# The attention output product as seven block products for eight, with its sums prepared in DRAM

## The chip, the cores and the metric

The kernel runs on one core of one Trainium2 chip. The metric is the device time of one execution in microseconds (us); lower is better. Before the change three runs gave 892.99, 893.65 and 893.84 us. A core has the engines TensorE (PE, with its weight loads shown as PEld), VectorE (DVE), ScalarE (ACT), GpSimd (POOL) and SyncE (SP). SP issues most transfers (DMAs); GpSimd issues those that add onto their destination.

## The reference, cut to what matters

One encoder layer on 512 tokens of width 1024, in float32: two mixers (a state-space scan and a gated spatial mixer), then cross-attention to 256 memory tokens, then a SwiGLU feed-forward layer of width 2816, each added onto the residual stream `h`, and a last norm.

```python
def memory_cross_attention(hn, memn, w_q, w_k, w_v, w_o):
    q = (hn @ w_q).reshape(bsz, seq, XATTN_HEADS, XATTN_HEAD_DIM)   # 4 heads of 256
    k = (memn @ w_k).reshape(bsz, MEM_LEN, XATTN_HEADS, XATTN_HEAD_DIM)
    v = (memn @ w_v).reshape(bsz, MEM_LEN, XATTN_HEADS, XATTN_HEAD_DIM)
    p = jax.nn.softmax(einsum('blhd,bmhd->bhlm', q, k) * XATTN_HEAD_DIM ** -0.5, axis=-1)
    o = jnp.einsum('bhlm,bmhd->blhd', p, v).reshape(bsz, seq, D_MODEL)
    return o @ w_o                                                  # w_xo, 1024 x 1024
...
h = h + memory_cross_attention(rms_norm(h, xattn_norm_g), memn, w_q, w_k, w_v, w_xo)
h = h + swiglu(rms_norm(h, ffn_norm_g), w_gate, w_up, w_down)
```

The change concerns `o @ w_o`, its addition onto `h`, and transfers for `w_q` and `w_down`.

## The kernel before, in words

**Three passes.** Each float32 operand is split into a high part (`split`, L85: a ScalarE cast to a shorter format) and a low part (L86: VectorE subtracts the high part). A product is three matmuls, high x high, high x low, low x high (`mm3`, L358). So each weight block costs TensorE matmuls, ScalarE one cast and VectorE one subtraction, and each product operand made on the chip the same pair.

**The plan of weights.** `plan` lists all weight blocks in the order of use. `next_w` hands out the next block, starts the loads of the blocks ahead of it (`LOADS` = 3 blocks; some 4 to 7) and splits up to `SPLITS` = 2 blocks ahead. A block of 128 x 1024 elements (512 KB) is loaded by SP into one of three `wraw` buffers and split into one of three `whi` and `wlo` pairs; some blocks have tiles of their own (`sums_place`). A `wraw` buffer is free when its split is done, a `whi`/`wlo` pair when its matmuls are done.

**Block products.** Several products (w_proj_b, w_q, gate and up, w_down) already use a scheme of the Strassen kind: the matrix is cut into 2 x 2 blocks, and seven products of sums of blocks take the place of eight. Sums of weight blocks that several steps need are made in DRAM by `plan_sums`: at plan entry j SP copies one block to DRAM scratch (L274, held in program order), and at entry j + step GpSimd's queue adds the other block by an accumulating transfer (L275). The list of pairs (j, step) fixes the entries.

**Order.** The program is written as one stream per stage; a scheduler orders each engine's queue at build time, from dependences and its own estimate of durations. Where the program says so (`in_order`), the written order is kept. On the chip each queue issues in its built order and an instruction waits for its operands.

**The stage around the change.** After the w_q product, `scores`, `turn` and `values` make each head's softmax, its transposes and its output; `values` splits the PSUM result into `ot_hi` and `ot_lo`. The w_xo product runs token by token, in two halves of 512 output columns: for the first half `tokm` holds four PSUM banks, for the four tiles of 128 tokens, while heads 1 to 3 are still made between its blocks (hooks `second` and `last_two`); the second half is a loop over token pairs. `add_evac` adds each finished bank onto `h` (L1294) and sums squares on ScalarE (L486). When a token tile has both halves, `feat_norm` norms it: GpSimd takes a root (`r`, L497), VectorE scales (`xs`, L512), TensorE transposes (`ptr`, L520), and ScalarE and VectorE split into `fn`, the operand of the feed-forward layer; `full` keeps the float32 value. The feed-forward stage begins with a remainder of 256 gate columns (`pf<-fn,s`) and the first unit (`px<-fn,whi`).

**Plan entries.** w_xo is plan entries 94 to 101; the feed-forward layer begins at 102.

## Time and profile before

| | |
|---|---|
| median of 3 runs | 893.65 us (892.99 to 893.84) |
| profiled execution | 893.12 us, span 891.3 us, granted TensorE clock 0.997 |
| instructions | 14796 |
| HBM read, written | 157.61 MB, 46.63 MB |

How to read the rows. A row of instructions gives start, duration, engine, line of the kernel, operation, result<-operands by the program's names, shapes, and xN when N follow one another; in brackets stands how long the engine had been idle before and what ended that. Durations of neighbours overlap a little, as instructions are pipelined. A row of waits gives the total in us, how often, and the longest. A row by stretch gives its bounds and length, then each engine's busy time with its number of instructions, the clock granted to TensorE, the mean busy share of the 16 DMA engines and GB/s. A row of transfers ends in the median us from issue to landing.

### The profile page before, as it was taken

What the parts mean: (1) busy time and instruction counts of PE and PEld (TensorE: products, weight loads), DVE (VectorE), ACT (ScalarE), POOL (GpSimd) and SP (SyncE); (2) the same over time, 40 slices, a digit from 0 to 9 for tenths busy, and PEclk for the clock granted to TensorE, in tenths of its full rate; (3) what the DMA queues carried; (4) which work ended last, traced back from release to release, by engine and by line L of the source; (5) the groups of instructions that cost most, each with busy time, mean ns of one, the idle gap of its engine ahead of it and who ended that gap; (6) DMA issues with size and microseconds to landing.
All of it is one profiled execution on the core that took longest, in us unless ns stands there. A gap on an engine that the chain in (4) does not pass through costs nothing.

```text
span 891.3 us, 14796 instructions
## 1 busy us (share of the span) xinstructions
PE 881.1 (99%) x5744; PEld 788.0 (88%) x5744; DVE 642.5 (72%) x1048; ACT 487.4 (55%) x714; POOL 106.9 (12%) x165
## 2 busy tenths in 40 slices
PE   9999999999999999999999999999999999999996
PEld 6788888888889998889899978999999999988875
DVE  5697653889847368658856836676878777899875
ACT  5743994244396254347656534645555455655664
POOL 1005301111032111001001001101121111000010
PEclk9999999999999999999999999999999999999998
DMA  8667456978533789834579747627899999356672
GB/s 255 196 189 182 114 155 177 189 191 190 159 87 84 212 285 268 288 117 140 168 221 256 194 103 197 166 81 181 213 237 233 216 225 249 95 167 207 204 230 102
DMA packets 118408, 165.36 MB, mean 186 GB/s; under 512 B 11825, under 2 KB 84161, under 8 KB 118210
## 3 DMA queue, kind: packets, MB, share of 16 engines
q1 hardware_dynamic: 97474, 135.74, 47.9%
q0 software_dynamic: 20576, 28.15, 19.9%
q8 instruction: 45, 0.74, 0.3%
q10 hardware_dynamic: 288, 0.52, 0.2%
q14 instruction: 25, 0.20, 0.1%
HBM read 157.61 MB, written 46.63 MB: 229 GB/s over the span
## 4 chain that ended last, share of the span: by engine, by line
PE 97%; DMA 1%; SPq 1%; ACT 0%; DVE 0%; issue 0%; POOLq 0%; ACTq 0%
PE pf L358 26%; PE pt L358 17%; PE px L1110 12%; PE dx L358 6%; PE pq L1110 6%; PE dq L358 3%; PE pv L1110 3%; PE bx L1110 3%; PE qx L1110 2%; PE dv L358 2%; PE pz L871 2%; PE pk L814 2%; PE bq L1110 1%; PE qv L1110 1%; PE psc L358 1%; PE qq L1110 1%
## 5 line engine op out<-in xcount | busy, mean ns | idle before, releaser
L86 DVE TENSOR_TENSOR wlo<-wraw,whi 128x1024 fp32r<-128x1024 f32 (+1 forms) x145 | 172.2, 1189 | 101.2 <-ACT whi L85 101.0
L85 ACT CAST whi<-wraw 128x1024 fp32r<-128x1024 f32 (+1 forms) x145 | 148.6, 1026 | 152.2 <-PE pf L358 44.0
L358 PE MATMUL pf<-xn,whi 128*128 128x512 f32 x448 | 139.6, 391 | 0.0
L358 PEld LDWEIGHTS pf<-xn,whi 128*128 128x128 f32 x448 | 83.7, 188 | 17.0
L358 PE MATMUL pf<-xn,wlo 128*128 128x512 f32 x224 | 87.3, 390 | 0.0
L1110 PE MATMUL px<-fn,whi 128*128 128x256 f32 x480 | 83.4, 277 | 0.0
L1110 PEld LDWEIGHTS px<-fn,whi 128*128 128x128 f32 x480 | 72.7, 188 | 0.2
L85 ACT CAST whi<-b 128x1024 fp32r<-128x1024 f32 x40 | 42.2, 1055 | 50.4 <-PE px L1110 27.4
L86 DVE TENSOR_TENSOR wlo<-b,whi 128x1024 fp32r<-128x1024 f32 x40 | 48.9, 1223 | 27.0 <-ACT whi L85 27.0
L1110 PE MATMUL px<-fn,wlo 128*128 128x256 f32 x240 | 66.4, 277 | 0.0
L1110 PE MATMUL pq<-s,whi 128*128 128x256 f32 x320 | 55.0, 276 | 0.0
L358 PE MATMUL dx<-whi,s 128*128 128x512 f32 x170 | 53.4, 390 | 0.4 <-DVE h L1734 0.4
L85 ACT CAST whi<-t 128x1024 fp32r<-128x1024 f32 x30 | 31.6, 1054 | 35.6 <-PE pv L1110 12.4
L86 DVE TENSOR_TENSOR wlo<-t,whi 128x1024 fp32r<-128x1024 f32 x30 | 36.7, 1225 | 19.7 <-ACT whi L85 19.7
L358 PEld LDWEIGHTS pf<-xn,wlo 128*128 128x128 f32 x224 | 42.1, 188 | 8.7
L1110 PEld LDWEIGHTS pq<-s,whi 128*128 128x128 f32 x320 | 48.3, 188 | 0.0
L1110 PEld LDWEIGHTS px<-fn,wlo 128*128 128x128 f32 x240 | 45.1, 188 | 0.0
L358 PE MATMUL pt<-whi,xn 128*128 128x512 f32 x128 | 43.7, 412 | 0.7 <-ACT xn L85 0.7
L1110 PE MATMUL pq<-s,wlo 128*128 128x256 f32 x160 | 44.2, 276 | 0.0
L358 PEld LDWEIGHTS dx<-whi,s 128*128 128x128 f32 x170 | 31.8, 188 | 7.5 <-issue 0.8
L358 PE MATMUL dx<-wlo,s 128*128 128x512 f32 x85 | 33.0, 390 | 0.0
L275 POOL DMA_DIRECT2D dsum<-in_w_down_dram x12 | 13.3, 1105 | 162.4 <-DMA dsum<-in_w_down_dram 162.4
(453 smaller groups left out, 2296.8 us busy)
## 6 DMA issues: line engine op xcount, KB each, us to landing
wraw<-in_w_in_dram SPq DMA_DIRECT2D x36, 512.0 KB, 4.7
dsum<-in_w_down_dram SPq DMA_DIRECT2D x20, 512.0 KB, 5.4
wraw<-dsum SPq DMA_DIRECT2D x20, 512.0 KB, 4.1
b<-in_w_gate_dram SPq DMA_DIRECT2D x15, 512.0 KB, 5.4
b<-in_w_up_dram SPq DMA_DIRECT2D x15, 512.0 KB, 5.3
wraw<-in_w_down_dram SPq DMA_DIRECT2D x15, 512.0 KB, 4.4
dsum<-in_w_down_dram POOLq DMA_DIRECT2D x10, 512.0 KB, 8.1
dsum<-dsum POOLq DMA_DIRECT2D x10, 512.0 KB, 8.5
```

Of the source, the lines that this page charges most:

```text
L85: hi = nc.scalar.copy(dst_hi, src)
L86: lo = nc.vector.tensor_tensor(dst_lo, src, dst_hi.bitcast(F32), ALU.subtract)
L275: plan[j + step][1].append((0, lambda d=dst, x=more: nc.gpsimd.dma_start(d, x, accum_op=ALU.add)))
L358: m = nc.tensor.matmul(ps, a[x], b[y], start=start and i == 0, stop=stop and i == 2, skip_group_check=free)
L814: nc.tensor.matmul(ps[32 * j:32 * j + 32, q, :], bd[i][:, g].rearrange("p d c -> p (d c)"), lc(es[i], g), start=(i == 0), stop=False, tile ...
L871: nc.tensor.matmul(ps[:, g, :], wt[:, g, :], u[:, o * GO + g, :], start=True, stop=True)
L1110: nc.tensor.matmul(ps[:, j, :], a[x], b[y], start=start and j == k == i == 0, stop=k == 3 and i == 2, skip_group_check=True)
```

## The change

w_xo is computed as one 2 x 2 block product over all 512 tokens. The attention output `o`, feature by token, is cut into four parts (features K0 and K1, tokens T0 and T1), w_xo into four blocks of 512 x 512, and seven products q = 1 to 7 are added onto `h` with signs. Each block of a product comes in two pieces c = 0, 1 of 256 rows, so there are 14 plan entries (`XO`) in place of 8. A piece is used for two token tiles. Four of the seven weight operands are sums, made in DRAM scratch `xsum` by eight new jobs of `plan_sums`; the other three are blocks of w_xo. The two pieces of the last product, q = 3, get tiles of their own.

`values` no longer splits the attention output: it copies it to `of`, and `attention_part` makes the operands of the seven products: two sums and four splits for heads 0 and 1, six sums and ten splits for heads 2 and 3. The operands of q = 5 and 6 lie in the tiles of the keys (`kt_hi`, `kt_lo`), which the scores have finished with. Products 6, 5, 4 and 3 go on accumulating in the banks of earlier products, so a bank is added onto `h` more than once. Tokens 0 and 1 are normed before tokens 2 and 3.

The jobs of `plan_sums` have new places. Two of w_q's eight jobs move ahead, under the w_in projections. w_down's 24 jobs are made in the order q = 5, 6, 7, 4 in place of 5, 7, 6, 4; eight of them used to come ahead of the feed-forward layer and now four do, so that two come early in its first jobs and the last ones are closer together. The feed-forward layer begins at plan entry 108.

```diff
+    XSRC = {1: (0, 0), 2: (1, 0), 3: (1, 1)}
+    xsum = {q: dp.tile([P, KD // 2, 512], F32, name=f"xsum{q}") for q in (4, 5, 6, 7)}
+    XO = ((1, 0), (7, 0), (1, 1), (7, 1), (6, 0), (5, 0), (6, 1), (5, 1), (4, 0), (4, 1), (2, 0), (2, 1), (3, 0), (3, 1))
...
+    def plan_xo():
+        for q, c in XO:
+            got, place = {}, 2 + 2 * c if q == 3 else None
+            def load(q=q, c=c, got=got):
+                got["raw"] = wp.tile([P, 2, 512], F32, tag="raw", name="wraw", bufs=3)
+                nc.sync.dma_start(got["raw"], xo_block(*XSRC[q], c) if q in XSRC else xo_sum(q, c))
+            plan.append(((w_xo, q, c), [(LOADS, load)], lambda got=got, place=place: halves(got.pop("raw"), place)))
...
+        for q, first, more in ((5, (0, 0), lambda c: xo_block(0, 1, c)), (7, (0, 1), lambda c: xo_block(1, 1, c)),
+                               (6, (1, 1), lambda c: xo_sum(5, c)), (4, (1, 0), lambda c: xo_sum(6, c))):
+            for c in range(2):
+                jobs.append((xo_sum(q, c), xo_block(*first, c), more(c)))
...
-    plan_sums([(5, 3), (7, 3), (9, 2), (13, 5), (14, 5), (16, 4)] + [(18 + 2 * i, 3) for i in range(8)] +
-              [(51 + 2 * i, 2) for i in range(4)] + [(85 + 3 * i, 3) for i in range(3)] +
-              [(95 + 2 * i, 2) for i in range(3)] + [(122 + 4 * i, 4) for i in range(16)])
+    plan_sums([(5, 3), (7, 3), (9, 2), (13, 5), (14, 5), (16, 4)] + [(i, 3) for i in (18, 20, 22, 23, 25, 26, 28, 29, 31, 32)] +
+              [(51 + 2 * i, 2) for i in range(5)] + [(i, 3) for i in (67, 74, 82, 87, 91, 95, 99, 118, 121)] +
+              [(124 + 4 * i, 4) for i in range(15)] + [(182 + 3 * i, 4) for i in range(3)])
...
-            split(ot_hi[:, 2 * hd + dt_, :], ot_lo[:, 2 * hd + dt_, :], ps)
+            nc.scalar.copy(of[:, 2 * hd + dt_, :], ps)
+        attention_part(hd)
...
+    def attention_part(hd):
+        u = slice(2 * (hd % 2), 2 * (hd % 2) + 2)
+        lw = slice(u.start + 4, u.stop + 4)
+        a11, a12, a21, a22 = (of[:, k, t] for t in (T1, T0) for k in (u, lw))
+        def operand(q, src):
+            split(xops[q][0][:, u], xops[q][1][:, u], src)
+        if hd < 2:
+            operand(1, a11)
+            s3_ = np_.tile([P, 2, 256], F32, tag="ev", name="s3", bufs=2)
+            nc.vector.tensor_tensor(s3_, a11, a21, ALU.subtract)
+            operand(7, s3_)
+            return
+        nc.vector.tensor_tensor(a21, a21, a22, ALU.subtract)
+        nc.vector.tensor_tensor(a11, a21, a11, ALU.subtract)
+        operand(6, a11)
+        operand(5, a21)
+        operand(4, a22)
+        operand(2, a12)
+        nc.vector.tensor_tensor(a12, a12, a11, ALU.add)
+        later(2, lambda: operand(3, a12))
...
+    def xo_product(ps, q, c, start, stop, w=None, ts=(0, 1)):
+        hi, lo = w or next_w(w_xo, q, c)
+        a = xops[q]
+        for t in ts:
+            tsl = slice(t * P, (t + 1) * P)
+            for k in range(2):
+                mm3(ps[t], (a[0][:, 2 * c + k, tsl], a[1][:, 2 * c + k, tsl]), (hi[:, k, :], lo[:, k, :]),
+                    start and k == 0, stop and k == 1, True)
+        tick(1.35 * len(ts))
...
-    tokm(w_xo, 0, ot, KD, add_evac(0, 1, None), hooks={1: second, 2: last_two})
+    ox = [bank("ox0"), bank("ox1")]
+    xo_product(ox, 1, 0, True, False)
+    values(1, *pts.pop(1))
+    turn(2, probs2)
+    oy = [bank("oy0"), aux("oy1")]
+    xo_product(oy, 7, 0, True, False)
+    values(2, *pts.pop(2))
+    turn(3, probs3)
+    xo_product(ox, 1, 1, False, True)
+    onto(ox, 2, 0, ALU.add)
+    values(3, *pts.pop(3))
+    xo_product(oy, 7, 1, False, True)
+    onto(oy, 0, 1, ALU.subtract)
+    oq = [bank("oq0"), bank("oq1")]
+    xo_product(ox, 6, 0, False, False)
+    xo_product(oq, 5, 0, True, False)
+    xo_product(ox, 6, 1, False, True)
+    onto(ox, 0, 1, ALU.subtract)
+    xo_product(oq, 5, 1, False, True)
...
+    onto(oq, 0, 1, ALU.add)
+    onto(ox, 0, 0, ALU.add)
...
+    onto(ox, 2, 1, ALU.subtract)
+    xo_product(oy, 4, 0, False, False)
+    xo_product(oy, 4, 1, False, True)
...
+    xo_product(ov, 2, 0, True, False)
+    xo_product(ov, 2, 1, False, True)
+    onto(ov, 2, 0, ALU.add)
...
+    ws = [next_w(w_xo, 3, c) for c in range(2)]
+    for t in range(2):
+        for c in range(2):
+            xo_product(oq, 3, c, False, c == 1, ws[c], (t,))
```

More of the change, by code (lines that the diff above doesn't have):

```diff
@@ L226, in plan_pair, with xo_block, xo_sum @@
             plan.append(((w, 512 * n, q), [(LOADS, load)], lambda got=got: halves(got.pop("raw"))))
+    XSRC = {1: (0, 0), 2: (1, 0), 3: (1, 1)}
+    xsum = {q: dp.tile([P, KD // 2, 512], F32, name=f"xsum{q}") for q in (4, 5, 6, 7)}
+    XO = ((1, 0), (7, 0), (1, 1), (7, 1), (6, 0), (5, 0), (6, 1), (5, 1), (4, 0), (4, 1), (2, 0), (2, 1), (3, 0), (3, 1))
+    def xo_block(i, j, c):
+        return block(w_xo, 4 * i + 2 * c, 2, 512 * j, 512)
+    def xo_sum(q, c):
+        return xsum[q][:, 2 * c:2 * c + 2, :]
+    def plan_xo():
[5 more added lines that the diff above has]
+            plan.append(((w_xo, q, c), [(LOADS, load)], lambda got=got, place=place: halves(got.pop("raw"), place)))
     def plan_units(units, down):
@@ L267, in plan_sums @@
                                  pair_block(w, *first, n), pair_block(w, *more, n)))
-        for q, i, jc, more in ((5, 0, 0, lambda c: down_block(0, 1, c)), (7, 0, 1, lambda c: down_block(1, 1, c)),
-                               (6, 1, 1, lambda c: down_sum(5, c)), (4, 1, 0, lambda c: down_sum(6, c))):
+        for q, first, more in ((5, (0, 0), lambda c: xo_block(0, 1, c)), (7, (0, 1), lambda c: xo_block(1, 1, c)),
+                               (6, (1, 1), lambda c: xo_sum(5, c)), (4, (1, 0), lambda c: xo_sum(6, c))):
+            for c in range(2):
+                jobs.append((xo_sum(q, c), xo_block(*first, c), more(c)))
+        for q, i, jc, more in ((5, 0, 0, lambda c: down_block(0, 1, c)), (6, 1, 1, lambda c: down_sum(5, c)),
+                               (7, 0, 1, lambda c: down_block(1, 1, c)), (4, 1, 0, lambda c: down_sum(6, c))):
             for c in range(CHUNKS):
@@ L315, in hybrid_layer_kernel @@
     plan_pair(w_q, qsum, False)
-    plan_tok(w_xo, 0, KD)
-    for i in range(4):
-        plan_block(w_xo, 2 * i, 2, 512, 512, place=(None, None, 2, 4)[i])
+    plan_xo()
     FS = 2560
@@ L1455, in hybrid_layer_kernel, with onto, half_done @@
     ot_lo = slot("E", (P, KD, T), F32R, "ot_lo")
+    of = slot("B", (P, KD, T), F32, "of")
+    ot_q = lambda ks, ts: (ot_hi[:, ks, ts], ot_lo[:, ks, ts])
+    xops = {1: ot_q(K0, T1), 2: ot_q(K1, T1), 4: ot_q(K1, T0), 7: ot_q(K0, T0), 3: ot_q(K0, T1)}
+    def attention_part(hd):
[18 more added lines that the diff above has]
+        later(2, lambda: operand(3, a12))
+    g_f = gain(ffn_norm_g[0], "g_f")
+    def xo_product(ps, q, c, start, stop, w=None, ts=(0, 1)):
[7 more added lines that the diff above has]
+        tick(1.35 * len(ts))
+    def onto(ps, t0, half, op):
+        for t in range(2):
+            hs = h[:, t0 + t, HALF[half]]
+            nc.vector.tensor_tensor(hs, hs, ps[t], op)
+    def half_done(t, half):
+        sum_sq(hss[:, 1, t, half:half + 1], h[:, t, HALF[half]])
     values(0, *pts.pop(0))
@@ L1458, in hybrid_layer_kernel @@
     probs3 = scores(3)
+    for q, nm in ((5, "kt_hi"), (6, "kt_lo")):
+        s_ = ap_.tile([P, KD, M], F32R, name=nm).rearrange("p (i k) t -> p i k t", i=2)
+        xops[q] = s_[:, 0], s_[:, 1]
     turn(1, probs1)
-    def second():
-        values(1, *pts.pop(1))
-        turn(2, probs2)
-        turn(3, probs3)
-    def last_two():
-        for i in (2, 3):
-            values(i, *pts.pop(i))
-    g_f = gain(ffn_norm_g[0], "g_f")
-    ot = (ot_hi, ot_lo)
-    fn_hi, fn_lo = token_slot("fn", AWAY)
-    fn = (fn_hi, fn_lo)
-    tokm(w_xo, 0, ot, KD, add_evac(0, 1, None), hooks={1: second, 2: last_two})
+    ox = [bank("ox0"), bank("ox1")]
[17 more added lines that the diff above has]
+    xo_product(oq, 5, 1, False, True)
     at.close()
@@ L1482, in hybrid_layer_kernel @@
     full = fp.tile([P, KD, T], F32, tag="full", name="full", bufs=1)
-    fin = add_evac(1, 1, feat_norm(g_f, fn_hi, fn_lo, full))
-    held = []
-    for t0 in (0, 2):
-        ps = {t: bank(f"pt{t - t0}") for t in (t0, t0 + 1)}
-        for wi in range(2):
-            if t0 == 0:
-                held.append((wi,) + next_w(w_xo, 2 * wi, 2, 512, 512))
-            for t in ps:
-                tok_block(ps[t], t, held[wi:wi + 1], ot, 2, slice(0, 512), wi == 0, False)
-            tick(2.7)
-        if t0 == 0:
-            held += [(wi,) + next_w(w_xo, 2 * wi, 2, 512, 512) for wi in (2, 3)]
-        for t in ps:
-            tok_block(ps[t], t, held[2:4], ot, 2, slice(0, 512), False, True)
-            fin(t, ps[t])
-            tick(2.7)
+    onto(oq, 0, 1, ALU.add)
+    onto(ox, 0, 0, ALU.add)
+    for t in range(2):
+        half_done(t, 1)
+    onto(ox, 2, 1, ALU.subtract)
+    xo_product(oy, 4, 0, False, False)
+    xo_product(oy, 4, 1, False, True)
+    fn_hi, fn_lo = token_slot("fn", AWAY)
+    fn = (fn_hi, fn_lo)
+    to_fn = feat_norm(g_f, fn_hi, fn_lo, full)
+    for t in range(2):
+        hs = h[:, t, HALF[0]]
+        nc.vector.tensor_tensor(hs, hs, oy[t], ALU.add)
+        half_done(t, 0)
+        to_fn(t, hss[:, 1, t, :])
+    ov = [bank("ov0"), bank("ov1")]
+    xo_product(ov, 2, 0, True, False)
+    xo_product(ov, 2, 1, False, True)
+    onto(ov, 2, 0, ALU.add)
+    for t in (2, 3):
+        half_done(t, 0)
+    ws = [next_w(w_xo, 3, c) for c in range(2)]
+    for t in range(2):
+        for c in range(2):
+            xo_product(oq, 3, c, False, c == 1, ws[c], (t,))
+        hs = h[:, 2 + t, HALF[1]]
+        nc.vector.tensor_tensor(hs, hs, oq[t], ALU.add)
+        half_done(2 + t, 1)
+        to_fn(2 + t, hss[:, 1, 2 + t, :])
     s3 = np_.tile([P, 4, 256], F32, tag="gain", name="s3", bufs=2)
```

## The prediction

> **What bounds the kernel now.** I read the page first, then busy time by stretch, the waits of the stage that the change rewrites, and single instructions for durations.

> ```profile
> span 891.3 us, 14796 instructions
> PE 881.1 (99%) x5744; PEld 788.0 (88%) x5744; DVE 642.5 (72%) x1048; ACT 487.4 (55%) x714; POOL 106.9 (12%) x165
> ...
> PE 97%; DMA 1%; SPq 1%; ACT 0%; DVE 0%; issue 0%; POOLq 0%; ACTq 0%
> ```

> TensorE (PE) is busy for 99% of the span, and 97% of the chain that ended last is its matmuls. Time is gained by fewer matmuls, and lost where TensorE begins to wait. The stretches show where it waits now:

> ```profile
> core 0: us, PE busy (x) PEld busy (x) DVE busy (x) ACT busy (x) POOL busy (x), PEclk, DMA share, GB/s
> 440.00:505.70 65.70, 65.70 (x511) 62.76 (x510) 44.91 (x69) 38.09 (x66) 4.29 (x4) 1.00 0.82 235
> 505.70:563.60 57.90, 56.96 (x267) 45.98 (x266) 32.27 (x56) 27.34 (x54) 5.31 (x6) 1.00 0.53 137
> 563.60:600.00 36.40, 36.40 (x318) 36.35 (x317) 27.71 (x32) 19.82 (x27) 1.87 (x2) 1.00 0.43 119
> 600.00:660.00 60.00, 60.00 (x532) 60.00 (x531) 44.51 (x44) 32.24 (x40) 8.27 (x7) 1.00 0.87 217
> 785.00:850.00 65.00, 65.00 (x288) 53.84 (x287) 56.72 (x68) 38.74 (x51) 0.81 (x1) 1.00 0.68 203
> 850.00:891.30 41.30, 34.02 (x157) 27.87 (x156) 28.05 (x40) 22.45 (x37) 5.76 (x8) 0.94 0.51 164
> ```

> The second row is the w_xo stage, from its first matmul to the first feed-forward one. TensorE is idle there for 0.94 us of 57.9; in the four full rows around it, for none. VectorE (DVE) works 32.27 us and so is idle for 25.6; ScalarE (ACT) works 27.34. TensorE's waits in the whole span (the second row is this stage's), then VectorE's in the stage, from 497 us on:

> ```profile
> PE idle L556 <- DVE mhalf L481: 1.1, 1, 1.1
> PE pt L358 <- ACT ot_hi L85: 0.9, 2, 0.7
> PE pt L358 <- ACT xn L85: 0.7, 1, 0.7
> PE dx L358 <- DVE h L1734: 0.4, 1, 0.4
> ```

> ```profile
> DVE ot_lo L86 <- ACT ot_hi L85: 11.5, 4, 3.5
> DVE wlo L86 <- ACT whi L85: 8.4, 5, 3.1
> DVE xs L512 <- POOL r L497: 1.8, 2, 1.0
> ```

> No wait of TensorE is for a load. VectorE's idle time is waiting for work that TensorE releases, through ScalarE's casts. Whether the change can use it is the question of this case.

> **The matmuls removed.** The old product has 8 weight blocks x 4 token tiles x 2 rows x 3 passes = 192 matmuls of 512 columns; the new one has 14 blocks x 2 x 2 x 3 = 168. Their pace, from the chain, and where the stage starts and ends:

> ```profile
> 536.38 17.32 PE pt L358 x76
> ```

> ```profile
> 505.72 0.39 PE L358 MATMUL pt<-whi,ot_hi 128*128 128x512 f32 x1
> ...
> 524.53 0.50 PE L358 MATMUL pt<-whi,ot_hi 128*128 128x512 f32 x1 [0.68 <-ACT ot_hi L85]
> ...
> 553.54 1.04 PE L520 MATMUL ptr<-ident,xs 128*128 128x128 f32 x8
> ...
> 563.93 2.64 PE L358 MATMUL pf<-fn,s 128*128 128x256 f32 x21
> ```

> 17.32/76 = 0.228 us each, so 24 fewer take off 5.5 us, all on the path. The 0.9 us of old waits go too: between a head's values and their use the new order has other matmuls.

> **The vector work added.** Durations (512 elements a row, then 1024, then the norm):

> ```profile
> 537.99 2.36 DVE L86 TENSOR_TENSOR s<-wraw,s 128x1024 fp32r<-128x1024 f32 x2 [0.26 <-ACT s L85]
> 540.27 1.88 DVE L1294 TENSOR_TENSOR h<-h,pt 128x512 f32<-128x512 f32 x3
> ...
> 549.75 1.42 DVE L512 SCALAR_TENSOR_TENSOR xs<-h,r,g_f 128x512 f32<-128x512 f32 x2 [0.75 <-POOL r L497]
> ...
> 559.89 0.68 DVE L86 TENSOR_TENSOR fn<-ptr,fn 128x512 fp32r<-128x512 f32 x1
> ```

> ```profile
> 490.01 1.08 ACT L85 CAST p_hi<-ppt 128x512 fp32r<-128x512 f32 x2
> ...
> 536.90 2.01 ACT L85 CAST s<-wraw 128x1024 fp32r<-128x1024 f32 x2
> ...
> 540.98 0.64 ACT L486 ACTIVATE sq<-h 128x512 f32<-128x512 f32 x1 [0.66 <-DVE h L1294]
> ```

> Six more weight blocks: 6 x 1.18 = 7.1 us on VectorE, 6 x 1.0 on ScalarE. Operands: 14 splits in place of 8 and eight sums of attention outputs: 14 x 0.63 = 8.8 us on VectorE; ScalarE keeps its eight PSUM reads as copies and gets 14 casts, 14 x 0.54 = 7.6. Adding products onto h: 18 additions in place of 8, 10 x 0.63 = 6.3. In all VectorE gets 22.2 us and ScalarE 13.6. Then VectorE has 54.5 us and ScalarE 40.9, in a stage that should take 52.4. ScalarE is covered; VectorE is not, except for what runs over into the next stretch, where it is idle for 8.7 us.

> **Where TensorE then waits.** I carried the three queues through by hand in the order in which the changed kernel issues them, on the old clock. First, `hi` and `lo` have three buffers, so the cast of block (5,1) waits until (6,0) is used up; TensorE has two matmuls (0.46 us) to do before it needs the cast (1.05 us, and hand-overs): 0.8 us of waiting. Behind it on ScalarE stand the cast of (4,0) and an operand's, which TensorE needs later still. Second, in front of the feed-forward layer. TensorE finishes (6,1), after 88 w_xo matmuls, 36 of attention values and 20 transposes, at 505.7 + 124 x 0.228 + 20 x 0.13 (1.04/8) + 0.8 = 537.4 at most. The cast of (4,1) ends at 538.5, but VectorE has six additions onto h queued before its half and finishes it at 541.5. Only then is there a raw buffer for (3,0). Its load:

> ```profile
> wraw<-qsum SPq DMA_DIRECT2D x8, 512.0 KB, 3.9
> wraw<-in_w_xo_dram SPq DMA_DIRECT2D x8, 512.0 KB, 6.2
> ```

> I take 5.0 us, between the two, as three loads for the first feed-forward unit go ahead of it on SP: it lands at 546.5 (behind it on SP are (3,1) and the first gate block, each wanted later). ScalarE casts by 547.6 and does two sums of squares by 549.0, GpSimd's root (0.56, below) gives r at 549.9. VectorE scales tokens 0 and 1 with one addition between (1.42 + 0.63 + 1.42) by 553.4, has four weight halves queued (4 x 1.18) till 558.1, then two halves of `fn`, an addition and the third half of `fn`, which the first gate product needs (2 x 0.68 + 0.63 + 0.68): 560.8. TensorE by its own work is there at 563.6 - 5.5 - 0.9 + 0.8 = 558.0, with 0.1 of leading matmuls: it waits 2.7 us. With a load of 3.9 us that is 1.6, with 6.2 it is 3.9. The other two tokens follow 12 us of TensorE work later and have room.

> **What I cost at nothing.** Eight w_xo sums in DRAM: SP issues eight copies more, GpSimd eight accumulating transfers more, and a queue can be held by them, as here, where one stands in front of the memory norm's root:

> ```profile
> 369.74 1.13 POOL L275 DMA_DIRECT2D dsum<-in_w_down_dram  x1 [5.72 <-DMA dsum<-in_w_down_dram]
> 370.46 1.01 POOL L497 TENSOR_TENSOR r<-ms,mhalf 128x1 f32<-128x1 f32 x1
> ...
> 549.16 0.56 POOL L497 TENSOR_TENSOR r<-ms,mhalf 128x1 f32<-128x1 f32 x1 [2.98 <-DVE ms L496]
> ```

> Now two stand there, 1 to 3 us more; the changed order has the transposes that need this root 13 or more matmuls (3 us) later, which covers it. Uncovered it would cost up to 3. Two w_q sums move under the w_in projections, where no load is waited for. Five w_down sums move: four more run under the feed-forward layer, early ones in the stretch at a DMA share of 0.43, a late one at 0.68, and between them the spacing stays; the price is 0 to 2. The six added loads (3 MB) lie in the stretch at 0.53. The second `oy` accumulator takes one of three auxiliary banks, so a turn's transposes alternate over two; other matmuls follow them, and without those it would cost one eviction, 0.54 + 0.63.

> **Sum.** -5.5 - 0.9 + 0.8 + 2.7 = -2.9. The profiled execution took 893.12 us, 0.53 below the median of 893.65; from the one I come to 890.2, from the other to 890.75, and give 890.5. Beyond the stage TensorE has no gap in which the gain could be lost.

> **Rivals.** *VectorE keeps up*: if the order hides the load and the 2.7 us go, 5.6 us are gained: about 887.9. For it: 25.6 us of idle time against 22.2. Against it: most of the idle time is early, while the additions are late.

> *VectorE falls behind* (the other side). If its idle time can't be filled, the third half of `fn` comes later than 560.8. The old one ended at 560.6 (the row at 559.89); with 22.2 us more and x us of idle time filled it ends at 560.6 + 22.2 - x. My walk is x = 22.0. TensorE's gain of 5.6 is used up at 563.6, x = 19.2, 75% of the 25.6. With 60% filled, x = 15.4: 567.4, slower by 3.8, about 897. For it: 11.5 us of the idle time is waiting for values that TensorE makes no sooner.

> *It cancels*: 70 to 80% filled gives about 893.

> *The array's clock drops*: the only row with a granted clock below 1.00 is the last, 0.94, with 7.3 us of TensorE idle; the w_xo row with its 0.68 us gap has 1.00. A pause in front of the feed-forward layer that grows toward that length could bring the same loss, 6% of 41.3 = 2.5 us: 893.0. [...]

> *The moved sums collide* with loads or roots: up to 5 us (3 at the root, 2 at w_down): 895.5.

> **Chances.** Forecast 0.42, VectorE keeps up 0.20, it cancels 0.14, clock 0.05, VectorE falls behind 0.13, sums 0.06. Within 0.2% (1.8 us, about what a measurement of this kernel can tell) lie the third and fourth. So faster 0.62, same 0.19, slower 0.19. The range goes from 5.6 + 0.8 gained, 887.2, to 895.3, short of the 897; the likeliest case alone: 889.4 to 891.7.

> **What would show it.** TensorE's sum of matmuls in the stage down by 24; a wait before the first gate product for `fn`'s low half, 1.5 to 4 us; a wait of under 1.2 us for a cast of `whi` some 27 us into the stage; VectorE busy over 90% of the stage; none in the w_out or w_down stretches. The prediction is wrong if TensorE waits in several places for attention operands, or if a later stretch shows idle time.

## The result, and the profile after

The changed kernel takes 904.09 us in the median (903.37 to 905.39) against 893.75 (892.99 to 894.92) on the same chip: a ratio of 1.012, with a 95% interval of 1.0105 to 1.0135. It is slower by 10.3 us where I had forecast 3.2 less. The profiled execution took 903.66 us, its span 901.7.

The page of the changed kernel, its first line, the busy times, and the engines' shares of the chain that ended last:

```profile
span 901.7 us, 14853 instructions
PE 887.2 (98%) x5720; PEld 793.6 (88%) x5720; DVE 663.1 (74%) x1078; ACT 498.5 (55%) x734; POOL 115.5 (13%) x173
...
PE 83%; DMA 7%; DVE 5%; ACT 2%; issue 2%; SPq 1%; POOLq 0%; POOL 0%; ACTq 0%; DVEq 0%
```

TensorE has its 24 matmuls less (5720 for 5744), and yet is busy for 6.1 us more. So the matmuls themselves became dearer on average. The stretches of the w_xo stage, of the gate and first unit, and of the units, their borders moved along with the work:

```profile
core 0: us, PE busy (x) PEld busy (x) DVE busy (x) ACT busy (x) POOL busy (x), PEclk, DMA share, GB/s
...
507.40:560.20 52.80, 51.04 (x239) 41.24 (x237) 47.48 (x79) 34.88 (x64) 3.56 (x4) 1.00 0.59 171
560.20:594.90 34.70, 32.72 (x262) 32.04 (x263) 26.96 (x34) 20.75 (x31) 4.42 (x5) 0.95 0.61 168
600.00:660.00 60.00, 60.00 (x511) 60.00 (x511) 43.74 (x43) 30.29 (x37) 8.27 (x8) 1.00 0.87 215
```

Read the third row against its twin of before, "600.00:660.00 ... 60.00 (x532)". Both say that TensorE is busy for all of the 60 us at a granted clock of 1.00. But it now gets through 511 matmuls and not 532, 4% fewer. Nothing in the busy share, the clock or the waits shows that; only the count does. The chain prints it in another way, as 24-matmul products in the feed-forward layer. First before, from the place where its pace changes on, then after:

```profile
573.99 2.83 PE pv L1110 x24
576.82 0.23 PE idle L1116
...
606.99 2.72 PE px L1110 x24
```

```profile
609.17 2.83 PE px L1134 x24
```

2.72/24 is 113.3 ns from start to start, 2.83/24 is 117.9 (117.7 over longer stretches). I call these the fast and the slow pace. TensorE's waits in the whole span after:

```profile
PE ptr L544 <- ACT full L548: 1.7, 1, 1.7
PE oq L382 <- DVE s L86: 1.6, 2, 1.1
...
PE qv L1134 <- ACT qv L1147: 0.8, 1, 0.8
...
PE dq L382 <- DVE wlo L86: 0.4, 1, 0.4
PE dq L382 <- ACT whi L85: 0.4, 1, 0.4
...
PE idle L1140 <- ACT fn L85: 0.3, 1, 0.3
PE pf L382 <- ACT fn L85: 0.2, 1, 0.2
```

Four instructions mark the stages: the first of w_xo, of the gate product, of the first unit's product 5, and of w_down. Before (the first of w_xo, at 505.72, and the gate, at 563.6, stand in the prediction), then after:

```profile
593.23 0.39 PE L1110 MATMUL pq<-s,whi 128*128 128x256 f32 x2
...
770.03 0.39 PE L358 MATMUL dx<-whi,s 128*128 128x512 f32 x1
```

```profile
507.39 0.39 PE L382 MATMUL ox<-whi,ot_hi 128*128 128x512 f32 x1
...
560.16 0.51 PE L382 MATMUL pf<-fn,s 128*128 128x256 f32 x2 [0.20 <-ACT fn L85]
...
594.87 0.40 PE L1134 MATMUL pq<-s,whi 128*128 128x256 f32 x2
...
778.60 0.40 PE L382 MATMUL dx<-whi,s 128*128 128x512 f32 x1
```

So the 10.4 us of span fall to the stages thus:

| Stage | before | after | difference |
|---|---|---|---|
| up to the first w_xo matmul | 505.7 | 507.4 | +1.7 |
| w_xo, to the first gate matmul | 57.9 | 52.8 | -5.1 |
| gate and first unit, to its product 5 | 29.6 | 34.7 | +5.1 |
| units, to w_down | 176.8 | 183.7 | +6.9 |
| w_down and the end | 121.3 | 123.1 | +1.8 |

The block product brought its 5.1 us. All of it was lost in the next 35 us, and three other losses came on top: 6.9 us among the units, 1.8 in w_down and 1.7 ahead of the w_xo stage.

### The profile page after: what moved, and what is told of

The parts are those of the page before. It is cut to its first block, busy times and chain, and to the rows that moved or that the text cites. A ratio compares the mean times of both kernels' runs of the same rounds, so it can differ in the third digit from the quotient of the medians.

```text
span 901.7 us, 14853 instructions
## 1 busy us (share of the span) xinstructions
PE 887.2 (98%) x5720; PEld 793.6 (88%) x5720; DVE 663.1 (74%) x1078; ACT 498.5 (55%) x734; POOL 115.5 (13%) x173
## 4 chain that ended last, share of the span: by engine, by line
PE 83%; DMA 7%; DVE 5%; ACT 2%; issue 2%; SPq 1%; POOLq 0%; POOL 0%; ACTq 0%; DVEq 0%
PE pf L382 24%; PE px L1134 12%; PE pt L382 10%; PE pq L1134 6%; PE dx L382 4%; PE pv L1134 3%; PE dq L382 3%; PE bx L1134 3%; DVE wlo L86 2%; DMA wraw<-in_w_v_dram 2%; DMA wraw<-dsum 2%; PE dv L382 2%; PE qx L1134 2%; PE pz L895 2%; PE pk L838 2%
## 5 line engine op out<-in xcount | busy, mean ns | idle before, releaser
L86 DVE TENSOR_TENSOR wlo<-wraw,whi 128x1024 fp32r<-128x1024 f32 (+1 forms) x151 | 179.4, 1189 | 96.3 <-ACT whi L85 95.6
L85 ACT CAST whi<-wraw 128x1024 fp32r<-128x1024 f32 (+1 forms) x151 | 154.6, 1025 | 163.4 <-PE pf L382 43.9
L1134 PE MATMUL px<-fn,whi 128*128 128x256 f32 x480 | 86.0, 281 | 0.0
L85 ACT CAST whi<-b 128x1024 fp32r<-128x1024 f32 x40 | 42.0, 1051 | 54.6 <-PE px L1134 29.8
L86 DVE TENSOR_TENSOR wlo<-b,whi 128x1024 fp32r<-128x1024 f32 x40 | 48.8, 1222 | 31.1 <-ACT whi L85 31.1
L1134 PE MATMUL pq<-s,whi 128*128 128x256 f32 x320 | 57.0, 281 | 0.0
L86 DVE TENSOR_TENSOR wlo<-t,whi 128x1024 fp32r<-128x1024 f32 x30 | 36.7, 1224 | 20.2 <-ACT whi L85 20.2
L85 ACT CAST whi<-t 128x1024 fp32r<-128x1024 f32 x30 | 31.6, 1052 | 34.0 <-PE pv L1134 11.6
L382 PEld LDWEIGHTS pt<-whi,xn 128*128 128x128 f32 x128 | 24.7, 195 | 6.2 <-ACT xn L85 1.0
## 6 DMA issues: line engine op xcount, KB each, us to landing
wraw<-in_w_in_dram SPq DMA_DIRECT2D x36, 512.0 KB, 4.9
dsum<-in_w_down_dram SPq DMA_DIRECT2D x20, 512.0 KB, 6.0
wraw<-dsum SPq DMA_DIRECT2D x20, 512.0 KB, 4.4
b<-in_w_gate_dram SPq DMA_DIRECT2D x15, 512.0 KB, 4.8
b<-in_w_up_dram SPq DMA_DIRECT2D x15, 512.0 KB, 5.3
wraw<-in_w_down_dram SPq DMA_DIRECT2D x15, 512.0 KB, 4.0
dsum<-in_w_down_dram POOLq DMA_DIRECT2D x10, 512.0 KB, 7.9
dsum<-dsum POOLq DMA_DIRECT2D x10, 512.0 KB, 6.7
```

Of the source, the lines that this page charges most:

```text
L85: hi = nc.scalar.copy(dst_hi, src)
L86: lo = nc.vector.tensor_tensor(dst_lo, src, dst_hi.bitcast(F32), ALU.subtract)
L382: m = nc.tensor.matmul(ps, a[x], b[y], start=start and i == 0, stop=stop and i == 2, skip_group_check=free)
L1134: nc.tensor.matmul(ps[:, j, :], a[x], b[y], start=start and j == k == i == 0, stop=k == 3 and i == 2, skip_group_check=True)
```

## The experiments

All times are medians in us; beside them the kernel before took 893.6 to 894.1.

**One dummy product decides 7 us.** Behind the first unit's second product the kernel issues one matmul of 512 columns whose result nobody reads (`idle_product`). In the trace of before the pace changes from slow to fast at it (576.66 us), in that of after from fast to slow (580.40). I left it out and doubled it, in both kernels.

```diff
-    idle_product(ops[1][0], fn_hi)        # a_none, b_none: no dummy
```

```diff
     idle_product(ops[1][0], fn_hi)
+    idle_product(ops[1][0], fn_hi)        # a_two, b_two: two in a row
```

After without the dummy:

> After, without the one dummy product of 512 columns that stands behind the first feed-forward unit. Theory S (TensorE has two paces for 256-column matmuls, about 113.3 and 117.7 ns, and this dummy turns one into the other; in after it turns the fast one into the slow one): the some 1,600 to 1,700 matmuls from 577 us to 790 us stay at 113.3 ns, 4.4 ns x 1,650 = 7.3 us less, so 904.1 - 7.3 = 896.8 us (896 to 898). Theory A (the slow pace comes from what else runs or where the operands lie: VectorE's writes, the transfers, the tiles' addresses): the pace stays 117.7 and the time falls by the dummy's own 0.23 us, 903.9 us.

Before without it:

> Before, without the same dummy product. Theory S: the pace of 117.8 ns that stands from 563 to 576 us is kept to 770 us and beyond it is reversed too; some 1,700 matmuls x 4.4 ns = 7.5 us more among the units, less up to 1 us among the w_down products if these turn fast: 900 to 902 us. Theory A: 893.5 us.

Measured: after without the dummy 895.59, 8.5 less than after; before without it 900.23, 6.7 more than before (ratio 1.0066, 1.0047 to 1.0084). The chain of the two, first after, then before, without the dummy:

```profile
608.76 2.72 PE px L1134 x24
```

```profile
607.78 2.83 PE px L1110 x24
```

The changed kernel is the fast one now and the old one the slow one. So the pace isn't a matter of the new tiles, their addresses or the new traffic; TensorE kept it for some 190 us (in the trace of before the fast one from 576.66 to 770.03 us), and whether the dummy stood there decided between the two. How it does so, the next runs ask. The two with two dummies:

> After, with the dummy product twice in a row. If each dummy toggles the pace (theory S, parity): two cancel, 113.3 ns from 577 us on, 897 us. If a dummy sets the slow pace whatever stood before (theory S, setting): 904.3 us. Theory A: 904.3 us.

> Before, with the dummy product twice. Theory S by parity: as without it, 900 to 902 us. Theory S by setting (the last thing ahead of the products decides): 894.0 us. Theory A: 894.0 us.

Measured: 897.88 (895.33 to 907.96; the profiled execution is fast) and 894.21, fast. In the two traces the pace behind the pair is fast, in after from the fast pace ahead of it, in before from the slow one. The wide spread of the first suggests that its executions did not all go one way; there is a trace of one only.

**Does a dummy turn the pace over, or set it?** Theory T says that a dummy turns over the pace that stands; theory L, that a dummy which waits for nothing leaves the fast pace, while one that waits leaves it open. Three kernels put a dummy into a stretch whose pace is known.

```diff
         product(q, u, 5, True, ops)
+        if i == 0:
+            idle_product(ops[1][0], fn_hi)   # a_late and b_late; b_late2 has two
```

> After, with a second dummy product 17 us later, behind the first product of the first unit, where nothing is waited for. Theory L: 117.7 ns from 577 to 597 us and 113.3 from there to 790 us: 904.1 + 0.2 - 193/0.1177 x 0.0044 = 897.1 us (896 to 898). If only the place right behind the transposes can set the pace: 904.3 us.

> Before, with one more dummy product behind the first product of the first feed-forward unit (596 us), where the pace is 113.3 ns and nothing is waited for. Theory T (a dummy turns over the pace that stands): 117.7 ns from 596 to 770 us, 174/0.1133 x 0.0044 = 6.8 us more: 900.5 us (899.5 to 901.5). Theory L (a dummy that waits for nothing leaves the fast pace): 893.9 us.

> Before, with two dummy products in a row at the same place. Theory T: two turns, fast again, 894.1 us. Theory L: 894.1 us. Should one of them be slow here, neither holds: then 900.5 us.

Measured: 898.52, 893.38 and 894.34; the first is 0.5 above its range. In after the pace was slow up to the added dummy and fast behind it. In before it was fast and stayed so, with one dummy and with two. The chain of before with one:

```profile
592.57 2.72 PE pq L1110 x24
595.29 0.23 PE idle L1116
...
606.41 2.72 PE px L1110 x24
```

So a dummy doesn't turn over what stands (theory T falls). Within a stretch of 256-column matmuls without waits, it left the fast pace behind in these three traces, whichever stood before. In after the dummy itself waits 0.26 us for the last part of `fn`. Two kernels were to tell whether that matters.

```diff
     for i in range(2):
         gate_part(i, T1)
+        if i == 0:
+            idle_product(ops[1][0], fn_hi)   # a_moved, for the line above the loop
```

> After, with the dummy product 12 matmuls later, where nothing that it reads is late. Theory L (a matmul that has to wait, even 0.3 us, leaves TensorE at the slow pace; a dummy that waits for nothing leaves it at the fast one): fast from 577 us on, 896.5 us (895 to 898). Theory T (the dummy turns over whatever pace stands): slow as in after, 904 us.

The scheduler put the dummy back at the same instruction, since it still reads the late part of `fn`. So this run is no test, only a second sample of after: 906.57, slow. The other reads the first half of the tokens alone:

```diff
-    nc.tensor.matmul(aux("idle"), x[:, 0, 0:P], y[:, 4, :], ...)
+    nc.tensor.matmul(aux("idle").rearrange("p (a t) -> p a t", a=2), x[:, 0, 0:P], y[:, 4:6, T0], ...)
```

> After, with the dummy reading the first half of the tokens alone, so that it waits for nothing; it then stands 4 matmuls behind the last transposes of this stretch, 18 ahead of its old place, and what waits some 0.3 us for the last part of fn is the first matmul of w_up. Theory L (a dummy that waits for nothing leaves the fast pace, a dummy that waits leaves it open): fast from 577 us on, 896.5 us (895 to 898). Theory L2 (it is any late matmul that can leave the slow pace, with the dummy or without): the late w_up matmul comes after the dummy, the pace is open again: 896.5 or 904. Theory T (the dummy turns the pace over): 904 us.

Measured: 904.99, slow. The instructions around the dummy:

```profile
578.40 0.60 PE L544 MATMUL ptr<-ident,xs 128*128 128x128 f32 x4
...
579.33 0.40 PE L1143 MATMUL idle<-fn 128*128 128x512 f32 x1
579.57 2.29 PE L382 MATMUL pf<-fn,s 128*128 128x256 f32 x18
```

It waits for nothing, and the 18 matmuls behind it are slow at once: (2.29 - 0.28)/17 is 118 ns, 0.28 being one matmul's own duration. The first matmul of w_up, which was to wait, doesn't in this trace, so no late operand explains it (theory L2 falls here). Theory L, that a dummy without a wait always leaves the fast pace, falls as well: four matmuls behind transposes it left the slow one. Nor is it the transposes alone. In c_best, the last run below, the same dummy stands two matmuls behind them, and the pace, slow until there (2.83 us for 24 matmuls in its chain), is fast behind it, (2.66 - 0.28)/21 = 113.3 ns:

```profile
571.58 0.60 PE L545 MATMUL ptr<-ident,xs 128*128 128x128 f32 x4
571.93 0.48 PE L383 MATMUL pf<-fn,s 128*128 128x256 f32 x2
572.25 0.39 PE L1144 MATMUL idle<-fn 128*128 128x512 f32 x1
572.48 2.66 PE L383 MATMUL pf<-fn,s 128*128 128x256 f32 x22
```

What in the sequence sets the pace stays open.

**The stage's gain and where it went.** At the end of the w_xo stage the trace of after shows TensorE waiting 0.4 us for the low half of block (3,0), 1.1 for that of (3,1), 0.2 for `fn` and 1.7 for an eviction (the copy `full`), and then a fall of the granted clock. The rows give TensorE's busy time, its clock and the DMA's numbers alone, first for the 3.41 us ahead of the fall, then for the 3.42 us of half clock:

```profile
559.88:563.29 3.41, 1.48 (x9) 1.00 0.59 201
563.29:566.71 3.42, 3.42 (x17) 0.50 0.17 43
```

Half of 3.4 us is 1.7 us of work. It isn't the amount of waiting alone that brings the fall. In a_late and a_early the wait ahead of these transposes is longer (2.4 and 2.3 us), and the clock stays at 1.00; a_late has a stretch as long as the one above with less work in it and no fall:

```profile
561.55:564.96 3.41, 0.99 (x7) 1.00 0.79 266
```

The traces show what the falls have in common. In each of the 18 the times between one change of the clock and the next are whole multiples of 3.41 us (in after it changes at 563.29, 566.71 and 897.80 us, 1 and 97 times 3.413 us apart). Counted in these steps, from 20 us on, each of the 25 falls follows a step in which TensorE was busy for at most 45% (43% at 563.29 and 9% at 897.80 in after, 40% at 886.50 in before), and none follows a step with 48% or more (in after and before every other step at full clock has at least 73%). The stretch of a_late lies across two steps, of 58 and 71%. So it was in part luck, good or bad, how the waits fell into the steps. In the chain the waiting begins with a load:

```profile
541.78 1.22 DVE wlo L86
...
543.02 6.42 DMA wraw<-in_w_xo_dram
...
549.51 1.06 ACT s L85
...
557.33 3.58 DMA wraw<-in_w_gate_dram
...
560.93 1.04 ACT s L85
561.97 0.49 ACT full L548
```

It is the walk of the prediction: the split of (4,1), the load of (3,0), its cast, and only behind that cast ScalarE's sums of squares, which had been ready since 548. The experiment keeps the sums in program order, ahead of the cast:

```diff
+    pinned[0] = True
     for t in range(2):
         hs = h[:, t, HALF[0]]
...
     xo_product(ov, 2, 0, True, False)
+    pinned[0] = False
```

> After, with the sums of squares of tokens 0 and 1 and the chain behind them kept in program order on ScalarE and VectorE, so that they go ahead of the cast of block (3,0), whose load ScalarE waits 3.44 us for. Theory W (the end of the stage is VectorE's queue behind a late load): fn comes 2.5 to 3 us earlier, the wait of 1.73 us ahead of the transposes and the half clock behind it (562 to 567 us, some 1.7 us lost) go, and the first feed-forward unit begins 2.5 to 4 us earlier; since the dummy product then waits for nothing, the pace of 113.3 ns should hold behind it as well (another 7 us): about 893 us, or 890 if nothing new waits; 900.5 if the pace stays slow. Rival V (VectorE is full whatever the order): the low half of block (3,0) is late in its place, TensorE waits 2 to 3 us for that instead and the stage is no shorter: 903 to 904 us, or 896 to 897 with the fast pace.

Measured: 892.12, and a ratio of 0.9978 (0.9961 to 0.9994), so this version of the change is faster than before, by 0.2%. From its first w_xo matmul to the first unit's product 5:

```profile
509.38 0.39 PE L382 MATMUL ox<-whi,ot_hi 128*128 128x512 f32 x1
...
591.62 0.39 PE L1134 MATMUL pq<-s,whi 128*128 128x256 f32 x2
```

That is 82.2 us, for 87.5 before as well as after: the gain of 5.1 to 5.3 us stays. The transposes' wait is gone, and the clock with it stays at 1.00:

```profile
562.00:564.00 2.00, 2.00 (x20) 1.00 0.25 84
564.00:566.00 2.00, 2.00 (x19) 1.00 0.02 4
```

Theory W holds and rival V falls (TensorE waits 0.8 us for a low half, not 2 to 3): VectorE had room, it was the order behind one late load. The pace was fast here although the dummy waits 0.3 us, one more sign that its wait alone doesn't decide. But this execution is 3.7 us late already at 509.38, and 2.2 of that are waits in the w_v and w_q stages, shown below.

**The moved and added sums.** Before with the moved sums alone:

```diff
-        for q, i, jc, more in ((5, ...), (7, ...), (6, ...), (4, ...)):      # w_down's order
+        for q, i, jc, more in ((5, ...), (6, ...), (7, ...), (4, ...)):
-    plan_sums([... (51 + 2 * i, 2) x4, (85 + 3 * i, 3) x3, (95 + 2 * i, 2) x3, (122 + 4 * i, 4) x16])
+    plan_sums([... 87, 91, 95, 99, 112, 115 (3), (118 + 4 * i, 4) x15, (176 + 3 * i, 4) x3])
```

> Before, with the sums in DRAM of w_proj_b, w_q and w_down at the places and in the order of after, and no w_xo sums and no block product. My prediction priced this at 0 to 2 us: 893.6 to 895.7. If the slow pace of after came with the moved sums (their traffic under the feed-forward layer): 899 to 901 us. If the 1.7 us that after loses among the w_down products is theirs: 895.3 us.

Measured: 894.92 (1.0013, 0.9995 to 1.0031), with the fast pace. New in its waits are 0.4 us (`dq`) and 0.2 us (`dx`) for low halves of w_down's blocks. That is the same kind of loss as in w_down after; its whole cost, about 1 us by the medians, can't be told from none. The w_xo sums, moved away from w_k, w_v and w_q:

```diff
-              [(51 + 2 * i, 2) for i in range(5)] + [(i, 3) for i in (67, 74, 82, 87, ...)] + ...
+              [(i, 3) for i in (38, 42, 46)] + [(51 + 2 * i, 2) for i in range(5)] + [(i, 3) for i in (87, ...)] + ...
```

> After, with the eight w_xo sums in DRAM moved forward, all under w_proj_b, w_proj_a and w_out, none under w_k, w_v and w_q. Theory Q (three of them crowd the loads of w_v and w_q, whose matmuls wait 0.2 to 2 us and turn slow for 2 us more): the first w_xo matmul comes at 505 to 506 us after the span's start, not at 507.4 to 509.4, and the time falls by 1.7 to 3 us as long as the pace in the feed-forward layer stays what it was: 901 to 902.5 us. If the moved order of loads alone is at fault: 904 us.

Measured: 905.85, and the first w_xo matmul comes at 509.42, no sooner. The waits of w_v and w_q went, but others came elsewhere, in the gated linear unit of the first mixer:

```profile
PE pf L383 <- ACT yg_hi L85: 2.1, 2, 1.5
```

I had placed the sums into a stretch with a lower DMA share (in before 0.56 from 256 to 316 us, for 0.68 in the whole span), where small transfers are under way and are waited for (`yd<-y`, 32 KB each; in after ScalarE's `yg_hi` waits 1.6 us for `ygt<-yd`, which reads what they write). GpSimd's queue shows how they came late:

```profile
315.14 1.19 POOL L301 DMA_DIRECT2D xsum<-in_w_xo_dram  x1 [12.56 <-DMA xsum<-in_w_xo_dram]
315.88 2.58 POOL L957 DMA_DIRECT2D yd<-y  x4
```

The accumulating transfer waits for its copy, and the small transfers `yd<-y`, on which `yg_hi` depends, stand behind it; in after they were issued from 312.02 on. It is the held queue that the prediction named for the root, at another place. The next leaves the sums out:

```diff
-                nc.sync.dma_start(got["raw"], xo_block(*XSRC[q], c) if q in XSRC else xo_sum(q, c))
+                nc.sync.dma_start(got["raw"], xo_block(*XSRC.get(q, (0, 0)), c))   # and no w_xo jobs in plan_sums
```

> After with the sums of squares in program order (a_pin), and without the eight w_xo sums in DRAM: blocks 4 to 7 are read from w_xo itself, so four of the seven products are of other weights than the reference's. Theory Q (the traffic of these sums delays the loads of w_v and w_q): the waits ahead of the w_xo stage go, its first matmul comes at 505 to 506 us and the time is 892.1 - 2 to 3.5 = 888.5 to 890 us. Rival: the waits stay with the changed order of the queues, 891.5 to 892.5 us.

Measured: 893.55 (0.9989, 0.9966 to 1.0013). There is no wait of TensorE between 340 us and the w_xo stage, as theory Q says, where a_pin has 2.2 us of them:

```profile
PE pt L382 <- ACT whi L85: 0.9, 1, 0.9
PE qv L1134 <- ACT qv L1147: 0.8, 1, 0.8
...
PE pt L382 <- DVE wlo L86: 0.5, 1, 0.5
```

One execution could miss them by chance: of the seven traces with the sums at their places in after, six have such waits, 0.9 to 2.6 us, and one (a_two) has none. But in the traces without these sums there, TensorE never waits at these matmuls, so theory Q is well supported. The times that I gave were wrong: the first w_xo matmul came at 506.78, with 2.0 us of waiting for `xn` at the start of the kernel, and the 2 us gained came back as other waits, 1.2 us more for halves of the blocks of q = 3 and 0.9 more in w_down. The wait for `xn` is between nothing and 2.2 us from trace to trace, so one trace can't tell a microsecond ahead of w_xo.

**Repairs together.** c_pin_early has a_pin, a_early and the dummy of a_t0; c_all also w_down's sums in the old order:

> After, with all three repairs: the sums of squares in program order (a_pin), the w_xo sums early (a_early), the dummy that waits for nothing (a_t0). If their gains add: 892.1 of a_pin less 2 to 3: 889 to 890.5 us, 3 to 4.5 below before. If the w_q loss was chance: 892 us.

> As the run before this one, with the w_down sums in the order of before and its spacing, as far as places are left. If the new order of these sums costs the 1.0 to 1.5 us that the moved sums cost alone, in before: 888 to 889.5 us. If any change of the order of vector work there costs the same: 889 to 890.5 us.

Measured: 895.27 and 894.84, worse than a_pin alone. The waits of c_all from 290 us on:

```profile
PE pf L383 <- ACT yg_hi L85: 3.4, 1, 3.4
PE oq L383 <- DVE s L86: 1.0, 1, 1.0
PE py L947 <- DMA yd<-y: 0.5, 1, 0.5
PE dx L383 <- DVE h L1834: 0.4, 1, 0.4
```

The 3.4 us are the badly placed sums again, and behind them the clock falls to half for 3.4 us in c_all and 6.8 in c_pin_early, which loses 1.7 and 3.4 us more. In w_down only the old wait for `h` is left, where c_pin_early still has the two new ones, so the order and places of its sums were the cause there. The last run moves three sums to where neither collision is:

```diff
-              [(i, 3) for i in (38, 42, 46)] + [(51 + 2 * i, 2) for i in range(5)] +
+              [(51 + 2 * i, 2) for i in range(5)] + [(i, 3) for i in (62, 65, 68)] +
```

> c_all with the last three w_xo sums between w_out and w_v and none under w_proj_b: the waits for yg_hi (3.4 us) go. If none comes in its place: 894.8 - 3.4 = 891.4 us, down to 889.5 if the loads of w_v are free as well. If each place under the memory's products costs as much: 892 to 893 us.

Measured: 888.96, 0.5 below its range, and a ratio of 0.9959 (0.9935 to 0.9984). Of the waits above only 1.0 us for `s` and 0.4 for `h` are left from 340 us on. Seven of the ten executions took 887.5 to 890.9 us, the other three 894.3 to 896.2. The trace is of one of the seven; the slow pace, worth 7 us, would explain the three, but that isn't shown.

So the block product, with the vector work in order, a fast pace and the sums in other places, is faster than both kernels, than before by 0.4% or 3.7 us (5.2 by the medians). For the change as it stood I had forecast 3.2.

## Why the prediction was wrong

*The matmuls removed*, -5.5: right, 24 fewer, and the stage became 5.1 us shorter. The old waits of 0.9 went too. In place of these 6.4 us the stage gained 5.1, as 1.6 us of new waits fall into it and four of its transposes (0.4) moved behind it.

*Where TensorE then waits*: the mechanism was right, the places were not. The 0.8 us for the cast of (5,1) did not come. The 2.7 us came as 1.6 for the low halves of (3,0) and (3,1), 0.2 for `fn` and 1.7 for an eviction behind the cast of a gate block: 3.5 in all, as the two terms' 3.5, and that the totals agree is luck. The load that starts it took 6.42 us, where I took 5.0 and had 6.2 as the bound. VectorE was busy for 47.48 of 52.8 us, the 90% that I named. The sign of being wrong that I gave came too: in the stretch behind the stage TensorE was idle for 2.0 us.

*The clock rival* came true in addition to the forecast, at 1.7 us where I had priced it at 2.5. I had expected it from a pause that grows toward the 7.3 us of idle time in the last stretch; how short a pause can cost the clock, no run had shown. In after the longest wait was 1.7 us, TensorE was busy for 1.48 of the 3.41 us ahead of the fall, and yet the clock fell. By the count over the 18 traces a step that was busy for 45% or less was enough. A single pause of 3.4 us, which I had no run for, came in c_all and c_pin_early, and the clock fell there too. With 2.0 us of waits after 560.2 (1.7 and the dummy's 0.3), 1.7 of clock and four more transposes (0.4), 4.1 of the 5.1 us that this stretch lost are named. Another 0.4 is the slow pace of its 96 matmuls behind the dummy (x 4.4 ns); the rest I have not split up.

*"Beyond the stage TensorE has no gap in which the gain could be lost"*: this is the step that failed, and it cost the most. Between the forecast of -2.9 and the +10.4 us of the span lie 13.3 us: 6.9 are this step, 2.9 the gain that I had forecast, which the stage brought and the stretch behind it took back, 1.8 w_down and 1.7 what lies ahead of w_xo. I took the duration of a matmul as fixed, because TensorE was full. A full TensorE can lose time without a gap: 176.8 us at 113.3 ns are about 1,560 matmuls, x 4.4 ns = 6.9 us, just what the units lost, and the runs without the dummy show that it is the pace. The profile of before had both paces in it: 2.83 and 2.72 us for 24 matmuls of 256 columns on the two sides of the dummy product. I had not asked what the dummy was for. From these two numbers the pace after the change could not have been foretold, but that a shift of the sequence might change it could. No rival of mine had this mechanism.

*Costed at nothing*: the eight w_xo sums. Three of them run under w_k, w_v and w_q, whose loads I had not named as queued behind them; in the trace of after waits of 0.8 and 0.2 us and some 18 us of slow pace behind the first (157 matmuls x 4.4 ns = 0.7) made 1.7 us. Without the sums those waits are gone. The 1.7 is one execution's: in the traces of the runs that leave this part as it is in after, the first w_xo matmul comes between 505.5 and 509.4 us. *The w_down sums*, 0 to 2 us: w_down lost 1.7 to 1.8, of which the run with these sums alone shows about 1, not clear of none; with the old order its new waits go. So the rival of the colliding sums came true in part, at other places than those that it named.

## What to carry to other kernels

Count the matmuls per microsecond, not only the busy share: where products of as many matmuls stand in a trace with two durations, ask which instruction lies between, before a change shifts what precedes it. When work is moved ahead of a full stage, look in each queue for a ready instruction behind one that waits for a load; here one pinned order kept a whole stage's gain. And a low DMA share doesn't show that a place is free: the sums in DRAM cost most here (3.4 us of waits for `yg_hi` in c_all and 2.1 in a_early, for 0.9 to 2.6, and once none, at their places in after) where the share was 0.56, small transfers are waited for, and some stand behind a sum in their queue (in a_early `yd<-y` until 315.88 us, for 312.02 in after).
